# Turning the convolution's blocks at once for two of four tiles

## The chip, the cores and the metric

The kernel runs on one core of a Trainium2 chip. Time is device time in microseconds of one execution, and the times shown are a median of several runs with the lowest and the highest. A core has five instruction queues that run beside each other: TensorE (PE, matrix products; PEld is its weight load), VectorE (DVE), ScalarE (ACT), GpSimd (POOL) and SyncE (SP), which here issues nearly all DMAs. Each queue takes its instructions in order, and an instruction that waits holds up all behind it on its engine. TensorE writes to PSUM, in banks of 128 rows by 512 values; the other data lie in SBUF as 128 rows (partitions).

## The reference

One decoder layer over 2048 rows of 1024 values. What matters here is the convolution group beside the attention group:

```python
    a, gate = jnp.split(u, 2, axis=-1)
    h = a * jax.nn.sigmoid(gate)
    h = lax.conv_general_dilated(
        h, conv_dw[:, None, :].astype(h.dtype), window_strides=(1,),
        padding=[(CONV_WIDTH - 1, 0)],
        dimension_numbers=("NWC", "WIO", "NWC"),
        feature_group_count=D_CONV) + conv_dw_b
    h = jax.nn.silu(layer_norm(h, conv_ln_g, conv_ln_b))
    return h @ w_conv_pw
```

Its result is joined with the attention's, goes through `w_out`, is normed and added to the input, and a dense SwiGLU block (width 2816) follows with its own norm. All is float32; products are made of three products of split operands.

## The kernel before

The 2048 rows are four tiles of 512 (t = 0 to 3). Stage A(t) makes the input projections of a tile, 14 groups of products (`proj`), and writes the gated values of the four blocks of 128 channels to DRAM (glu_scr). Beside it run other stages as side lanes: B(t) is the attention (tags tr, p, kz, ql), U folds the pointwise weights of the convolution into w_out, C(t) is the convolution, W(t) is the output projection with the norms. After them come the stages H, F and G, the SwiGLU block, for tiles 0 and 1 and then for 2 and 3. In the profile a buffer's name carries its stage: fc@C is a buffer of tag fc used by stage C.

The convolution of a tile has two parts.

- `stage_taps(t)` (line 554) works with channels as partitions. For each block c of 128 channels it loads the gated values (glu@C), makes y (fc@C, 128 x 512) with one multiply and 30 multiply-adds on VectorE, all recorded as line 94, and stores y to y_scr in DRAM (line 565).
- `stage_tail(t)` (line 568) loads the four blocks back (line 577) and turns them (`turner`, line 545): four transposes of 128 x 128 on TensorE into the one bank ct (line 549), and a copy by ScalarE into 128 columns of each of the four quarters of yt (line 550). yt then has rows as partitions and 512 channels beside each other.
- `conv_tail` (line 583) takes mean and variance over the channels (line 589), an inverse root on GpSimd, norms in place (line 597), and for each block c turns it back (line 601, bank ct again), makes tanh th and the linear value v in two buffers fc (lines 603, 605), joins them on VectorE (line 606) and stores v to mixT in DRAM (line 607).

mixT holds the eight blocks of 128 values that W(t) multiplies with w_out: four of the attention (line 520) and four of the convolution. W(1), after stage A, loads the attention's four blocks of tile 1 into a buffer of tag yt (line 705) and splits them (hl@W, line 708).

How many buffers a tag has is fixed: glu 2, fc 3, yt 1, ct one bank, tr three banks, mm four. A buffer is given on when the last instruction that uses it is done, a store to DRAM when it has landed.

The order on each engine is made when the program is built. A planner takes the instructions by priority, which follows the order in which they are written out, and by its own clock of when operands and buffers are ready. Main stages run through generators that say how long a piece takes; each lane gets credit at its rate (0.7 for the taps of tile 0, 1.1 for tile 1, lane `lc`; 2.0 for the tails of tiles 0 and 1, lane `ld`), and writes out pieces while it has credit. The taps are written with a priority 100 places behind and are tied to projections so as to keep pace (`dve`, line 92). A tail begins at least CS = 10 of these units after its taps (line 1368). By these rates tile 0's tail is written out while the first block of tile 1 is, and tile 1's second block comes behind it.

Of the kernel before, what the change touches and what calls it, by code (L numbers as in the profile page):

```python
# [17 lines left out]
AF = mybir.ActivationFunctionType  # L18
ALU = mybir.AluOpType
# [6 lines left out]
P = 128  # L26
T = 512
# [10 lines left out]
def layer_kernel(ctx, tc, x, xT, cols, rows, sinks, relb, onehot, w_in, w_pw, w_out, w_gate, w_up, w_down, out):  # L38
    nc = tc.nc
# [9 lines left out]
    def nm(s):  # L49
        uid[0] += 1  # L50
        return f"{s}@{lab[0]}_{uid[0]}"
# [3 lines left out]
    def t_(tag, shape, dt=F32):  # L55
        return sb.tile(list(shape), dt, tag=tag, name=nm(tag), bufs=BUFS[tag])
# [4 lines left out]
    def f2(tag, shape=(P, T)):  # L61
        return t_(tag, shape)
# [4 lines left out]
    def sm(n, dt=F32):  # L67
        kind = "A" if lab[0][0] == "G" else lab[0][0]
        return sb.tile([P, 8], dt, tag="sm" + kind, name=nm("sm"), bufs=16)[:, 0:n]
# [9 lines left out]
    act = nc.scalar.activation  # L79
# [12 lines left out]
    def dve(op):  # L92
        def emit(*args, **kw):
            r = op(*args, **kw)  # L94
            if not paced[0]:
                pace["main"] = r.ins
            elif pace["main"] is not None and pace["main"] is not pace["tied"]:
                tc.add_manual_dep(
                    r.ins,
                    pace["main"].name,  # L100
                    mybir.DependencyInfo(mybir.DependencyClass.NoSync, mybir.DependencyReason.DATA),
                    reason="conv taps keep pace with the projections",
                )
                pace["tied"] = pace["main"]
            if paced[0] and made["rows"]:
                made["new"] = True
                tc.add_manual_dep(
                    r.ins,
                    made["rows"][min(made["at"], len(made["rows"]) - 1)].name,
                    mybir.DependencyInfo(mybir.DependencyClass.NoSync, mybir.DependencyReason.DATA),  # L110
                    reason="conv taps keep pace with the products",
                )
                made["at"] += TIE
            return r

        return emit

    stt = dve(nc.vector.scalar_tensor_tensor)
# [25 lines left out]
    def rsqrt(ssq, n, mean_over, beside_taps=True):  # L144
        v = sm(n)
        y = sm(n)
        t = sm(n)
        vts(v, ssq, 1.0 / mean_over, EPS, ALU.mult, ALU.add)
        vts(y.bitcast(I32), v.bitcast(I32), 1, None, ALU.logical_shift_right)
        vts(y.bitcast(I32), y.bitcast(I32), -1, 0x5F3759DF, ALU.mult, ALU.add)  # L150
        for _ in range(3):
            if beside_taps:
                ptt(t, y, y, ALU.mult)
                ptt(t, t, v, ALU.mult)
                nc.gpsimd.tensor_scalar(t, t, -0.5, 1.5, ALU.mult, ALU.add)
                ptt(y, t, y, ALU.mult)
            else:
                vtt(t, y, y, ALU.mult)
                stt(t, v, -0.5, t, ALU.mult, ALU.mult)
                stt(y, t, 1.5, y, ALU.add, ALU.mult)  # L160
        return y
# [56 lines left out]
    lnh = cst.tile([P, 8], F32, name="lnh")  # L218
# [6 lines left out]
    mixT = dr.tile([KC, P, S], F32, name="mixT")  # L225
# [17 lines left out]
    y_scr = dr.tile([4, P, S], F32, name="y_scr")  # L243
# [290 lines left out]
    def conv_in(t, c):  # L534
        g = t_("glu", (P, 576))[:, 0 : HALO + T]
        if t == 0:
            nc.vector.memset(g[:, 0:HALO], 0.0)
            nc.sync.dma_start(g[:, HALO:], glu_scr[c, :, 0:T])
        else:
            nc.sync.dma_start(g, glu_scr[c, :, t * T - HALO : (t + 1) * T])  # L540
        y = f2("fc")
        vts(y, g[:, 0:T], dwh[:, c, 0:1], dwb[:, c : c + 1], ALU.mult, ALU.add)
        return g, y

    def turner(yt, ycs):
        def turn(c):
            b = ct()
            for s in range(4):
                nc.tensor.transpose(b[:, s * P : (s + 1) * P], ycs[c][:, s * P : (s + 1) * P], ident)
            act(yt[:, :, c * P : (c + 1) * P], b.rearrange("p (s c) -> p s c", c=P), AF.Copy)  # L550

        return turn

    def stage_taps(t):
        L = f"C{t}"
        for c in range(4):
            while f"g{t}{c}" not in started:
                yield None
            lab[0] = L
            g, y = conv_in(t, c)  # L560
            for j in range(1, TAPS):
                stt(y, g[:, j : j + T], dwh[:, c, j : j + 1], y, ALU.mult, ALU.add)
                yield 0.68
                lab[0] = L
            nc.sync.dma_start(y_scr[c, :, t * T : (t + 1) * T], y)
            yield 0.68

    def stage_tail(t):
        L = f"C{t}"
        lab[0] = L  # L570
        yt = t_("yt", (P, 4, 4 * P))
        ycs = []
        turn = turner(yt, ycs)
        for c in range(4):
            lab[0] = L
            y = f2("fc")
            nc.sync.dma_start(y, y_scr[c, :, t * T : (t + 1) * T])
            ycs.append(y)
            turn(c)
            yield 0.5  # L580
        yield from conv_tail(t, yt)

    def conv_tail(t, yt):
        L = f"C{t}"
        lab[0] = L
        mv = sm(8).rearrange("p (s a) -> p s a", a=2)
        for s in range(4):
            st = sm(6)
            nc.vector.bn_stats(st, yt[:, s])
            nc.vector.bn_aggr(mv[:, s], st)  # L590
        r = rsqrt(mv[:, :, 1], 4, 1.0)
        nmr = sm(4)
        stt(nmr, mv[:, :, 0], -1.0, r, ALU.mult, ALU.mult)
        yield YL if t < 2 else YL2
        lab[0] = L
        for s in range(4):
            act(yt[:, s], yt[:, s], AF.Identity, scale=r[:, s : s + 1], bias=nmr[:, s : s + 1])
        for c in range(4):
            b = ct()
            for s in range(4):  # L600
                nc.tensor.transpose(b[:, s * P : (s + 1) * P], yt[:, s, c * P : (c + 1) * P], ident)
            th = f2("fc")
            act(th, b, AF.Tanh, scale=lnh[:, c : c + 1], bias=lnh[:, 4 + c : 5 + c])
            v = f2("fc")
            act(v, b, AF.Identity, scale=lnh[:, c : c + 1], bias=lnh[:, 4 + c : 5 + c])
            stt(v, th, 1.0, v, ALU.add, ALU.mult)
            nc.sync.dma_start(mixT[4 + c, :, t * T : (t + 1) * T], v)
            yield YZ
            lab[0] = L

# [33 lines left out]
    bias = []  # L644
# [720 lines left out]
    for t in range(NT):  # L1365
        lc.add(f"T{t}", stage_taps(t))
    for t in range(2):
        ld.add(f"C{t}", stage_tail(t), lambda t=t: since(lc, f"T{t}", CS))
# [51 lines left out]
    lc.rates["T3"] = RC3  # L1420
    ws, ops = (2, 3), {}
    lw.add("C2", stage_tail(2))
    lw.add("W2", stage_w(2, "mid", ["ql", "chl"], ["chl", "yt"], tr))
    lw.add("C3", stage_tail(3), lambda: since(lc, "T3", CS))
    lw.add("W3", stage_w(3, "mid", ["ql", "chl"], ["chl", "yt"], tr, norm=lambda g: lw.add("N3", g)))
    lw.add("B11.2", stage_h_plain(ws, ops, "B11", 0))
# [71 lines left out]
```

## Time and profile before

| | |
|---|---|
| median of 3 runs | 1985.41 us (1983.29 to 1989.4) |
| profiled execution | 1988.67 us, span 1986.6 us |
| mean granted TensorE clock | 0.992 |
| taps of tile 0, first to last | 44.3 to 236.4 us of the span |
| taps of tile 1, first to last | 181.8 to 430.4 us |
| tail of tile 0, first load to last store | 180.9 to 292.4 us |
| tail of tile 1, first load to last store | 363.3 to 486.9 us |
| stage A, last product | about 485 us |

The span goes from the first to the last instruction of one execution recorded by the profiler. Busy times of engines overlap. A wait is given with the engine and line that waited and what ended it; "mm@A L85" is an instruction on tag mm in stage A that line 85 recorded. PEclk is the share of the full TensorE clock that was granted in a stretch.

### The profile page before, as it was taken

Reading aid. Unit: us, or ns where it says so; the run is one execution under the profiler, and the core shown is the slowest. Engines: PE = TensorE matmul, PEld = TensorE weight load, DVE = VectorE, ACT = ScalarE, POOL = GpSimd, SP = SyncE. Lnnn points to the kernel's source line nnn. Section 1 sums busy time; section 2 is a strip of 40 time slices with the busy share of each in tenths; the row PEclk is TensorE's granted clock in tenths of the full one; section 3 lists DMA queues with packets and bytes.
Section 4 is the critical chain, followed back from the end, with each engine's and each line's share of the span. In section 5 each row is a group of like instructions: output and inputs, shape, how many; then the busy total and the mean of one; then the engine's idle time right before and its main releaser. Section 6 shows DMA issues by size and latency. Waiting matters only on the chain.

```text
span 1986.6 us, 26669 instructions
## 1 busy us (share of the span) xinstructions
PE 1930.2 (97%) x8730; PEld 1542.3 (78%) x8730; DVE 1460.2 (73%) x2578; ACT 955.2 (48%) x1878; POOL 336.4 (17%) x415
## 2 busy tenths in 40 slices
PE   8999999998999999899999999989999999999997
PEld 6777767776777778778888778768888888888886
DVE  5999969986875898888658975766666665455557
ACT  5455454436737633334355466556634433345443
POOL 4011111003121200000000110144423332311003
PEclk9999999999999999999999999989999999999999
DMA  8797757669659867885477788797844542466664
GB/s 312 253 316 234 228 176 242 213 198 306 203 191 353 290 216 237 285 267 181 154 236 251 266 302 282 270 315 244 289 149 165 170 164 81 143 232 194 210 196 144
DMA packets 229403, 454.56 MB, mean 229 GB/s; under 512 B 22632, under 2 KB 48400, under 8 KB 229264
## 3 DMA queue, kind: packets, MB, share of 16 engines
q1 hardware_dynamic: 211024, 426.64, 64.5%
q10 hardware_dynamic: 18240, 26.22, 3.6%
q8 instruction: 69, 1.13, 0.2%
q14 instruction: 70, 0.57, 0.1%
HBM read 331.65 MB, written 121.12 MB: 228 GB/s over the span
## 4 chain that ended last, share of the span: by engine, by line
PE 43%; DMA 10%; DVE 9%; issue 3%; POOL 2%; ACT 2%; SPq 1%; DVEq 0%; ACTq 0%; POOLq 0%
PE mm@F L85 29%; PE mm@G L85 12%; DVE fc@C L94 2%; PE tr@W L85 2%; DMA gb@F<-keeps 1%; DVE hl@G L94 1%; DMA mids<-fa@F 1%; DMA fa@G<-mids 1%; DMA td<-fc@G 1%; DVE w@F L94 1%; DMA fc@G<-w_down 1%; DMA wx@G<-w_down 1%; DVE fa@F L94 1%; DVE chl@F L94 1%; DMA mixT<-fc@C 1%
## 5 line engine op out<-in xcount | busy, mean ns | idle before, releaser
L94 DVE SCALAR_TENSOR_TENSOR fc@C<-glu@C,colt,fc@C 128x512 f32<-128x512 f32 x480 | 356.5, 760 | 2.9
L85 PE MATMUL mm@F<-hl@H,w@F 128*128 128x512 f32 x1056 | 253.0, 390 | 3.3 <-ACT mm@F L919 2.0
L85 PE MATMUL mm@G<-hl@G,hl@G 128*128 128x512 f32 x924 | 232.6, 397 | 11.2 <-ACT hl@G L792 7.7
L85 PEld LDWEIGHTS mm@F<-hl@H,w@F 128*128 128x128 f32 x1056 | 197.5, 188 | 46.3 <-ACT mm@F L919 3.7
L85 PEld LDWEIGHTS mm@G<-hl@G,hl@G 128*128 128x128 f32 x924 | 173.0, 190 | 51.7 <-ACT hl@G L792 9.0
L85 PE MATMUL mm@A<-hl@A,w@A 128*128 128x512 f32 x840 | 206.5, 395 | 4.2 <-ACT w@A L127 1.9
L792 ACT ACTIVATE w@F<-chl@F 128x512 fp32r<-128x512 f32 x220 | 135.4, 625 | 142.1 <-PE mm@F L85 131.5
L85 PE MATMUL mm@G<-w@G,hl@G 128*128 128x512 f32 x876 | 199.4, 389 | 0.0
L85 PEld LDWEIGHTS mm@G<-w@G,hl@G 128*128 128x128 f32 x876 | 164.4, 188 | 34.1
L85 PEld LDWEIGHTS mm@A<-hl@A,w@A 128*128 128x128 f32 x840 | 155.4, 188 | 42.2 <-ACT w@A L127 2.6
L94 DVE TENSOR_TENSOR w@F<-chl@F,w@F 128x512 fp32r<-128x512 f32 x198 | 144.8, 735 | 35.9 <-ACT w@F L792 35.3
L85 PE MATMUL mm@F<-ql@H,w@F 128*128 128x512 f32 x528 | 128.4, 391 | 9.2 <-ACT mm@F L1026 5.0
L85 PE MATMUL mm@F<-mid@H,w@F 128*128 128x512 f32 x528 | 131.7, 396 | 0.0
L85 PE MATMUL mm@F<-p@H,w@F 128*128 128x512 f32 x528 | 129.4, 390 | 0.0
L85 PE MATMUL mm@F<-x@H,w@F 128*128 128x512 f32 x528 | 125.7, 391 | 0.0
L85 PEld LDWEIGHTS mm@F<-ql@H,w@F 128*128 128x128 f32 x528 | 98.8, 188 | 31.6 <-ACT mm@F L1026 6.4
L494 POOL TENSOR_SCALAR_AFFINE_SELECT p@B<-p@B 128x512 f32<-128x512 f32 x62 | 57.6, 938 | 374.0 <-ACT p@B L492 372.7
L85 PEld LDWEIGHTS mm@F<-mid@H,w@F 128*128 128x128 f32 x528 | 100.0, 190 | 21.9 <-ACT fa@F L1047 0.5
L85 PEld LDWEIGHTS mm@F<-p@H,w@F 128*128 128x128 f32 x528 | 99.5, 188 | 21.0 <-ACT at@F L1040 0.2
L85 PEld LDWEIGHTS mm@F<-x@H,w@F 128*128 128x128 f32 x528 | 98.6, 188 | 21.5 <-issue 0.8
L127 ACT ACTIVATE w@A<-raw@A 128x512 fp32r<-128x512 f32 x110 | 67.4, 625 | 93.5 <-PE mm@A L85 54.8
L94 DVE TENSOR_TENSOR w@G<-raw@G,w@G 128x512 fp32r<-128x512 f32 x73 | 51.5, 705 | 68.1 <-ACT w@G L792 66.8
(302 smaller groups left out, 3300.6 us busy)
## 6 DMA issues: line engine op xcount, KB each, us to landing
mids<-fa@F SPq DMA_DIRECT2D x154, 256.0 KB, 2.8
raw@A<-w_in SPq DMA_DIRECT2D x55, 512.0 KB, 4.7
w@A<-lo_in SPq DMA_DIRECT2D x84, 256.0 KB, 3.6
fc@G<-mids SPq DMA_DIRECT2D x77, 256.0 KB, 3.5
fa@G<-mids SPq DMA_DIRECT2D x75, 256.0 KB, 4.6
gb@F<-keeps SPq DMA_DIRECT2D x72, 256.0 KB, 3.9
w@W<-fold SPq DMA_DIRECT2D x32, 512.0 KB, 5.1
chl@F<-w_gate SPq DMA_DIRECT2D x22, 512.0 KB, 4.1
```

Of the source, the lines that this page charges most:

```text
L85: r = nc.tensor.matmul(*args, **kw)
L94: r = op(*args, **kw)
L127: act(w[:, 0], raw, AF.Copy)
L494: nc.gpsimd.affine_select(out=pg[:, kb].rearrange("p (i q) -> p i q", q=P), in_=pg[:, 1].rearrange("p (i q) -> p i q", q=P), compare_op=AL ...
L792: act(w[:, 0], x, AF.Copy)
```

## The change

For tiles 0 and 1 a finished block y is no longer stored to y_scr and loaded back. `stage_taps` takes the tile's yt when its first block is done, and turns each block right behind its last tap. `stage_tail` for these tiles then starts with `conv_tail`. In `conv_tail`, for all four tiles, the value v is written into the 128 columns of yt that were just turned back, no longer into a buffer fc, and the store to mixT reads it there. Tiles 2 and 3 still go through y_scr.

```diff
+    turns = {}
+
     def stage_taps(t):
...
-            nc.sync.dma_start(y_scr[c, :, t * T : (t + 1) * T], y)
+            if t < 2:
+                if c == 0:
+                    turns[t] = t_("yt", (P, 4, 4 * P))
+                turner(turns[t], {c: y})(c)
+            else:
+                nc.sync.dma_start(y_scr[c, :, t * T : (t + 1) * T], y)
             yield 0.68
 
     def stage_tail(t):
         L = f"C{t}"
         lab[0] = L
+        if t < 2:
+            yield from conv_tail(t, turns[t])
+            return
...
-            v = f2("fc")
-            act(v, b, AF.Identity, scale=lnh[:, c : c + 1], bias=lnh[:, 4 + c : 5 + c])
-            stt(v, th, 1.0, v, ALU.add, ALU.mult)
-            nc.sync.dma_start(mixT[4 + c, :, t * T : (t + 1) * T], v)
+            v = yt[:, :, c * P : (c + 1) * P]
+            four = lambda a: a.rearrange("p (s c) -> p s c", c=P)
+            act(v, four(b), AF.Identity, scale=lnh[:, c : c + 1], bias=lnh[:, 4 + c : 5 + c])
+            stt(v, four(th), 1.0, v, ALU.add, ALU.mult)
+            nc.sync.dma_start(four(mixT[4 + c, :, t * T : (t + 1) * T]), v)
             yield YZ
```

The counts of taps, transposes and of ScalarE's and VectorE's instructions stay as they are.

## The prediction

> **What bounds the kernel now.** I read the page's sums first, then the busy time by stretch, then who waits for whom, then the order of time around the waits.
>
> ```profile
> span 1986.6 us, 26669 instructions
> PE 1930.2 (97%) x8730; PEld 1542.3 (78%) x8730; DVE 1460.2 (73%) x2578; ACT 955.2 (48%) x1878; POOL 336.4 (17%) x415
> ```
>
> TensorE is busy in all but 56 us. Nothing in the change takes a matmul away, so all that it can win or lose are gaps of TensorE. Where they lie is shown by the busy time in stretches (columns: length, busy time of PE, PEld, DVE, ACT, POOL, then PE's clock, DMA share, GB/s):
>
> ```profile
> 44.00:245.00 201.00, 198.25 (x966) 153.58 (x966) 192.97 (x410) 96.50 (x228) 20.42 (x29) 1.00 0.77 258
> ...
> 250.00:284.00 34.00, 34.00 (x158) 23.95 (x157) 15.68 (x46) 19.65 (x47) 6.50 (x17) 1.00 0.54 175
> ...
> 481.00:490.00 9.00, 4.87 (x30) 3.71 (x29) 6.27 (x11) 3.57 (x7) 0.00 (x0) 0.88 1.04 396
> 490.00:495.00 5.00, 3.55 (x17) 3.02 (x18) 4.96 (x16) 2.19 (x4) 0.00 (x0) 0.52 1.08 362
> 495.00:560.00 65.00, 65.00 (x312) 46.39 (x311) 51.90 (x132) 38.24 (x102) 8.20 (x8) 1.00 0.67 220
> 560.00:1986.00 1426.00, 1385.66 (x6134) 1133.08 (x6132) 992.03 (x1550) 667.44 (x1211) 244.78 (x264) 0.99 0.67 223
> ```
>
> The convolution of tiles 0 and 1 runs from 44 to 487 us. In it TensorE is full but for one hole, 481 to 495, where it lacks 4.13 + 1.45 = 5.6 us and what it does is done at half clock (0.52). The list of waits names it, and what the turned loads cost today:
>
> ```profile
> PE tr@B L85 <- DVE sm@B L454: 5.6, 1, 5.6
> ...
> PE ct@C L549 <- DMA fc@C<-y_scr: 1.4, 2, 1.0
> ```
>
> The hole in order of time (start, length, engine; in brackets the idle time before it and what ended it):
>
> ```profile
> 476.66 0.38 SPq L607 DMA_DIRECT2D mixT<-fc@C  x1
> ...
> 480.55 0.37 SPq L705 DMA_DIRECT2D yt@W<-mixT  x1
> ...
> 483.66 0.55 DVE L94 TENSOR_SCALAR fc@C<-glu@C,colt 128x512 f32<-128x512 f32 x1 [7.43 <-DMA mixT<-fc@C]
> ...
> 486.17 0.68 DVE L94 SCALAR_TENSOR_TENSOR fc@C<-fc@C,fc@C 128x512 f32<-128x512 f32 x1
> ...
> 486.88 0.33 SPq L607 DMA_DIRECT2D mixT<-fc@C  x1
> ...
> 490.69 1.67 ACT L708 ACTIVATE hl@W<-yt@W 128x512 fp32r<-128x512 f32 x3 [4.69 <-DMA yt@W<-mixT]
> ...
> 491.45 1.65 PE L85 MATMUL tr@B<-kz,ql@A 64*128 64x256 f32 x12 [5.59 <-DVE sm@B L454]
> ...
> 493.03 7.45 PE L85 MATMUL mm@W<-w@W,hl@W 128*128 128x512 f32 x28
> ```
>
> Two chains end here. First, VectorE stands 7.43 us before the first instruction of a block of tile 2: its buffer (tag fc, three of them) is still being stored to mixT by tile 1's tail (issued 476.66). Work queued behind it, the score reductions of B3 that free the banks tr, comes late, and TensorE waits 5.59 us. Second, output projection W1 needs its activations: their load into yt goes out at 480.55, right after the tail's last transposes out of yt, ScalarE gets them at 490.69, and the products start at 493.03. Mending the first chain alone brings little.
>
> **The change part by part.** *The round trip through y_scr.* Eight stores and eight loads go (issues per line, SP's own, for all 16 of the four tiles; last column the median time to landing):
>
> ```profile
> y_scr<-fc@C SPq DMA_DIRECT2D x16, 256.0 KB, 3.3
> mixT<-at@B ACTq DMA_DIRECT2D x16, 256.0 KB, 2.5
> fc@C<-y_scr SPq DMA_DIRECT2D x16, 256.0 KB, 4.8
> mixT<-fc@C SPq DMA_DIRECT2D x16, 256.0 KB, 5.2
> ```
>
> That is 16 x 256 KB = 4.2 MB and 16 places in SP's queue; the transfers were beside other work, so the bytes are worth nothing by themselves. What counts is how long the turn stood behind the last tap:
>
> ```profile
> 236.38 0.32 SPq L565 DMA_DIRECT2D y_scr<-fc@C  x1
> ...
> 244.08 0.66 PE L549 MATMUL ct@C<-ident,fc@C 128*128 128x128 f32 x4 [1.04 <-DMA fc@C<-y_scr]
> ...
> 284.06 0.61 DVE L94 TENSOR_SCALAR fc@C<-glu@C,colt 128x512 f32<-128x512 f32 x1 [5.69 <-DMA mixT<-fc@C]
> ...
> 288.67 1.64 PE L85 MATMUL mm@U<-chl@U,mid@U 128*128 128x512 f32 x6 [0.79 <-DVE chl@U L94]
> ...
> 298.10 2.08 PE L85 MATMUL mm@A<-hl@A,w@A 128*128 128x512 f32 x8 [0.63 <-DVE mb@U L94]
> ```
>
> ```profile
> 430.43 0.32 SPq L565 DMA_DIRECT2D y_scr<-fc@C  x1
> ...
> 439.28 0.65 PE L549 MATMUL ct@C<-ident,fc@C 128*128 128x128 f32 x4
> ...
> 452.78 2.93 ACT L597 ACTIVATE yt@C<-yt@C,sm@C,sm@C 128x512 f32<-128x512 f32 x4 [0.57 <-DVE sm@C L94]
> ```
>
> Tile 0: 244.08 - 236.38 = 7.7 us; tile 1: 439.28 - 430.43 = 8.85 us. Without DRAM the transposes stand in TensorE's queue where the plan has the block finished. How far TensorE is behind VectorE there, I take from a pair of the same form, the normalised probabilities and their transposes:
>
> ```profile
> 198.75 1.28 DVE L94 TENSOR_TENSOR p@B<-p@B,sm@B 128x512 f32<-128x512 f32 x2
> ...
> 203.67 0.60 PE L491 MATMUL tr@B<-ident,p@B 128*128 128x128 f32 x4
> ```
>
> 203.67 - 200.03 = 3.6 us. So the tails start 7.7 - 3.6 = 4.1 and 8.85 - 3.6 = 5.2 us earlier, counted from the last tap.
>
> *The turns themselves.* The same 32 transposes and 8 copies as before, moved ahead in TensorE's and ScalarE's queues:
>
> ```profile
> L549 PE MATMUL ct@C<-ident,fc@C x64: 270/272/329, 193.2 to 1187.5; 128*128 128x128 f32 x64
> ...
> L550 ACT ACTIVATE yt@C<-ct@C x16: 577/597/600, 195.4 to 1187.8; 128x512 f32<-128x512 f32 x16
> ...
> L605 ACT ACTIVATE fc@C<-ct@C,lnh x16: 763/772/783, 266.8 to 1221.8; 128x512 f32<-128x512 f32 x16
> ```
>
> Their busy time is unchanged: 0. New is that each group waits for taps on VectorE and not for a load. From below that costs 0 (TensorE is 3.6 us behind), from above the 1.04 us of the one turn that did make TensorE wait, eight times: 8.3 us. I take 0.2 us each, 1.6 in all, nearer to the pair's row; VectorE is full there (192.97 of 201 us), so it isn't nothing. Behind a waiting transpose stand the projections of stage A, all of TensorE's work.
>
> *Values into the columns of yt.* L550 already writes such columns (597 ns), so L605 keeps its 772 ns. For VectorE's multiply no row has columns; between 0 and double its time, 8 x 0.68 = 5.4 us in two tails, it lies on an engine with 18.3 us to spare in 250 to 284: 0. The stores of mixT go out in runs of 512 B, not 2 KB. ScalarE's stores of at into the same mixT have such runs and land in 2.5 us, the tail's in 5.2, so 0; the ends are 2.5 and, as the longest store-like row here, the 10.1 us from 480.55 to 490.69.
>
> The Trainium skill speaks against this part: DMA: Bandwidth & Descriptors, Why small descriptors are slow (HBM only), gives a fixed overhead of about 3 cycles per packet beside 32-byte beats. By it a 512-byte run would cost 19 cycles for 16 and a 2 KB run 67 for 64, an estimate of some 13% more, or 0.7 us on a landing of 5.2; the row of at does not bear it out.
>
> *Buffers.* The tail takes four buffers of fc, not twelve, and none of them waits for a store. VectorE's waits of 5.69 and 7.43 us end. Tile 1's second block, written out in the plan behind tile 0's tail, starts earlier than 284.06 by the 4.1 us and by the 5.69; VectorE has the room (15.68 of 34 us busy). I take 6 us of it as surviving to tile 1's last tap: 424 for 430.43. In return the block finished first in tile 1 keeps its buffer until tile 0's last store has landed and yt is free (about 285): one buffer of three, and the tail needs one.
>
> In the tails of tiles 2 and 3 only the columns change. The buffer yt is next wanted there by a load of the very values that the tail stores, which waits for their landing anyway: 0.
>
> *The new wait.* yt is now held until the store of tile 1's last piece has landed, and W1's load of yt comes behind it. Today that piece is made at 486.17. Earlier taps take 6 us off, the missing round trip 5.2, and of VectorE's 7.43 us I count 3: made at 472, stored at 473, landed (5.2) at 478, against 480.55 for the load today. With its own 10.1 us the load arrives at 488; TensorE would be ready at 485.86 + 1.65 = 487.5 (the end of its work before the gap, 491.45 - 5.59, and the 12 score products). What is late next is thus this load, by 0.5 us; I take 1.2 with what follows on ScalarE.
>
> *Sum.* Hole at 491: -5.6. Half clock: 3.55 us of work at 0.52 becomes 1.85: -1.7. The waits of 1.04, 0.79 and 0.63, all behind the loads and VectorE's wait: -2.5. Turns +1.6, load of yt +1.2. Together -7.0 us. The profiled execution took 1988.67 us (span 1986.6 and 2.1 around it), so 1981.7 for its like; it is 3.3 us above the median of the runs, 1985.41, from which I forecast 1978.4.
>
> **The rivals.** *yt is let go too late (slower).* If tile 1's tail doesn't move, its last store is issued at 486.88 and lands at 492.1; the load goes 11.5 us later than now, the products of W1 start at 504.6, and the gap is 17 us for 5.8: with the small waits gone 1985.4 + 11.3 - 2.5 = 1994.2. It decides when that landing passes 480.55; it already eats the gain from about 477.4 (487.5 - 10.1). For it: not to lose I need 11.5 of the 14.2 us that I put together (6 + 5.2 + 3), and the tail's last two stores stand 10 us apart today (476.66, 486.88). Against it: both waits for mixT are gone for certain.
>
> *The hole stays.* The landing falls near 480: TensorE stops at W1's products, not at tr, and starts them at 493 as now. Only the 2.5 us less the 1.6 of turns are won: 1984.5.
>
> *Turns stop TensorE (slower).* If VectorE is behind the plan by x at each of eight turns, 8x is lost; at x = 1.1 the gain is gone (7.0 + 1.6 over 8), at the 7.7 us of the round trip it would be 60 us. With 2 us: 1978.4 - 1.6 + 16 = 1992.8. For it: VectorE is 96% busy until 245. Against it: TensorE never waits for VectorE in that stretch, by the list.
>
> *Another plan behind it.* All buffers and times of the plan from 245 us on shift, and the 40.3 us that TensorE lacks from 560 on (1426 - 1385.66) fall anew. Nothing says which way; a sixth of them, 6 us, either side: 1972 or 1984 on top of the forecast.
>
> **How the numbers follow.** From no change a measurement of this kernel tells about 0.3%, 6 us. Forecast as worked out 0.42 (own range 1974 to 1982; 0.33 over the bound, 0.09 within it); yt too late 0.15, slower; the hole stays 0.12, the same; turns stop TensorE 0.14 (0.10 slower, 0.04 the same); another plan 0.17 (0.08 faster, 0.04 the same, 0.05 slower). Faster 0.41, same 0.29, slower 0.30. The range: low 1972 from the better plan, high 1995 to take in yt too late and two microseconds at each turn.
>
> **What would show it.** In the changed kernel's profile: no wait of VectorE for mixT before 500 us; transposes of the turn within some 4 us of the last tap, TensorE's waits at them under 2 us in sum; tile 1's last tap before 428; the load of yt for W1 out before 480; no gap over 2 us and no clock under 1.0 between 481 and 495. Wrong it would be by a load of yt later than 481, by waits of TensorE for taps of a microsecond and more, or by gaps from 560 on over 46 us.

## The result, and the profile after

The changed kernel took 1998.0 us (median of 5, 1993.83 to 1998.56), the kernel before 1987.25 (median of 5, 1983.29 to 1989.4): a ratio of 1.0058, 95% interval 1.0043 to 1.0073. It is slower by 0.6%; the forecast was 1978.4. The profiled execution took 1996.4 us. The first line of the page, and the busy time by stretch (length, then PE, PEld, DVE, ACT, POOL, PE's clock, DMA share, GB/s), changed kernel:

```profile
span 1994.5 us, 26648 instructions
```

```profile
44.00:245.00 201.00, 200.98 (x978) 155.54 (x978) 193.80 (x409) 96.69 (x230) 18.96 (x31) 1.00 0.75 250
245.00:350.00 105.00, 105.00 (x498) 76.77 (x497) 85.92 (x198) 55.24 (x131) 16.70 (x27) 1.00 0.64 209
350.00:430.00 80.00, 80.00 (x383) 59.03 (x383) 75.04 (x174) 29.23 (x86) 6.93 (x8) 1.00 0.58 183
478.00:484.00 6.00, 4.44 (x40) 3.27 (x40) 4.88 (x23) 3.73 (x7) 0.00 (x0) 0.94 0.99 378
484.00:502.00 18.00, 8.39 (x44) 6.30 (x43) 12.41 (x35) 8.31 (x26) 0.00 (x0) 0.50 0.91 283
502.00:508.00 6.00, 6.00 (x18) 4.77 (x18) 5.29 (x16) 4.04 (x8) 1.63 (x2) 0.56 0.40 137
...
560.00:1994.00 1434.00, 1393.68 (x6157) 1139.80 (x6156) 993.36 (x1555) 668.81 (x1213) 245.76 (x264) 0.99 0.67 223
```

The same view of the kernel before, in the stretches of the hole, and before it:

```profile
245.00:350.00 105.00, 103.58 (x492) 75.24 (x490) 86.01 (x190) 55.53 (x130) 17.40 (x28) 1.00 0.65 214
350.00:430.00 80.00, 79.42 (x369) 57.22 (x366) 72.70 (x163) 30.40 (x88) 6.89 (x8) 1.00 0.63 202
478.00:484.00 6.00, 6.00 (x30) 4.96 (x29) 0.34 (x1) 5.42 (x8) 0.00 (x0) 1.00 1.01 395
484.00:502.00 18.00, 12.41 (x65) 9.35 (x63) 17.82 (x45) 6.11 (x21) 0.00 (x0) 0.81 0.92 312
502.00:508.00 6.00, 6.00 (x36) 4.86 (x34) 5.96 (x20) 6.00 (x15) 0.00 (x0) 1.00 0.69 242
```

Two things are to be seen. Up to 430 us the change does more than it was given: TensorE lacks 0.02 us from 44 to 430, where it lacked 4.75 (2.75, 1.42 and 0.58), so the turns cost it nothing. Then the hole is not closed but doubled: from 478 to 508 TensorE lacks 11.2 us instead of 5.6, and its clock is at half. Counted in work at full clock (busy time by clock, an estimate), those 30 us held 6.00 + 12.41 x 0.81 + 6.00 = 22.05 us before and 4.44 x 0.94 + 8.39 x 0.50 + 6.00 x 0.56 = 11.73 now. That is 10.3 lost; less the 4.7 won it leaves 5.6.

The hole in order of time, changed kernel (start, length, engine; in brackets the idle time and what ended it):

```profile
484.23 2.02 SPq L799 DMA_DIRECT2D fa@H<-hn_scr  x4
484.94 0.68 DVE L94 SCALAR_TENSOR_TENSOR yt@C<-fc@C,yt@C 128x512 f32<-128x512 f32 x1
...
488.94 0.98 SPq L618 DMA_DIRECT2D mixT<-yt@C  x1
...
495.61 0.36 SPq L716 DMA_DIRECT2D yt@W<-mixT  x1
...
500.99 2.19 ACT L719 ACTIVATE hl@W<-yt@W 128x512 fp32r<-128x512 f32 x4 [4.37 <-DMA yt@W<-mixT]
501.67 3.78 PE L85 MATMUL mm@W<-w@W,hl@W 128*128 128x512 f32 x8 [4.11 <-ACT hl@W L719]
```

VectorE's waits for mixT are gone. But W1's load of yt goes out at 495.61 instead of 480.55, behind the landing of tile 1's last store (issued 488.94), and W1's first product starts at 501.67 instead of 493.03. That store's value was made at 485.6 (484.94 + 0.68) and lay 3.3 us: SP's queue stood behind the loads fa@H of stage H (484.23), which had waited 4.0 us for stores to hn_scr (in DRAM) to land.

Behind the hole, two marks show the rest: the first transpose of stage H into tr, and the first product of stage G.

```profile
637.06 0.60 PE L810 MATMUL tr@H<-ident,fc@H 128*128 128x128 f32 x4
1012.95 1.52 PE L85 MATMUL mm@G<-hl@G,hl@G 128*128 128x512 f32 x6
```

```profile
642.63 0.60 PE L821 MATMUL tr@H<-ident,fc@H 128*128 128x128 f32 x4
1024.36 0.84 PE L85 MATMUL mm@G<-hl@G,hl@G 128*128 128x512 f32 x3
```

The first fence is before, the second after. To the first mark the changed kernel loses 5.6 us, the hole; from mark to mark 381.7 us stand for 375.9, another 5.8, in a stage that the change doesn't touch; and from there to the end it wins 3.5 back (spans 1994.5 and 1986.6).

### The profile page after: what moved, and what is told of

Same layout as the page of the kernel before. It is cut to its first block, busy times and chain, and to the rows that moved or that the text cites. A ratio compares the mean times of both kernels' runs of the same rounds, so it can differ in the third digit from the quotient of the medians.

```text
span 1994.5 us, 26648 instructions
## 1 busy us (share of the span) xinstructions
PE 1937.1 (97%) x8730; PEld 1549.0 (78%) x8730; DVE 1460.4 (73%) x2578; ACT 953.7 (48%) x1878; POOL 334.8 (17%) x415
## 4 chain that ended last, share of the span: by engine, by line
PE 74%; DMA 10%; DVE 10%; issue 3%; POOL 2%; ACT 1%; SPq 1%; DVEq 0%; ACTq 0%; POOLq 0%
PE mm@F L85 33%; PE mm@A L85 15%; PE mm@G L85 11%; PE mm@W L85 5%; PE tr@B L85 4%; DVE fc@C L94 2%; PE tr@W L85 2%; DVE hl@G L94 1%; DMA mids<-fa@F 1%; PE mm@U L85 1%; DMA fa@G<-mids 1%; DMA td<-fc@G 1%; DVE w@F L94 1%; PE tr@B L491 1%; DMA mixT<-yt@C 1%
```

## The experiments

Theory H: the loss is yt, held until tile 1's last store has landed. Rivals: theory T, the turns put tile 1's taps late, so the hole opens wherever v goes; and theory F, the planner's order behind 580 us came out worse by chance.

**The turns alone (e1).** v goes back into a buffer fc in all tails.

```diff
-            v = yt[:, :, c * P : (c + 1) * P]
+            v = f2("fc")
```

> The turns at once are kept, the values v of all tails go into a buffer fc as before the change. Theory H (yt held): the loss at 483 to 508 comes from yt being kept until tile 1's last store of mixT has landed. Then the load of yt for W1 goes out right behind tile 1's last back-transposes (482 in the changed kernel, not 495.6), W1's first product starts some 12 us earlier, the time TensorE lacks between 478 and 508 falls from 11.2 us (6 - 4.44 and 18 - 8.39) to 6 or less, and the time is 1988 to 1992. Theory T (the turns at once put tile 1's taps late, last tap 441 for 430): the load still comes by 482, but the waits of VectorE for mixT are back, and the time is 1992 to 1998. Theory F (the stages behind 640 were planned anew and cost 5.5 us): gaps from 560 on stay within 6 us of the changed kernel's or fall elsewhere, and the time may come out either side by that much.

2001.13 us, ratio 1.0059 (1.0044 to 1.0074). Theory H's numbers were not met, and the time lies above the ranges of both H and T, although TensorE lacks only 6.8 us from 478 to 508 (23.23 of 30 us busy) for the changed kernel's 11.2. The last turn of tile 1 came at 449.16 (441.34 in the changed kernel), and yt was held all the same, in another way: the tail's pieces waited for buffers fc that were still being stored.

```profile
491.98 0.78 ACT L615 ACTIVATE fc@C<-ct@C,lnh 128x512 f32<-128x512 f32 x1 [1.34 <-DMA mixT<-fc@C]
...
492.81 1.11 PE L611 MATMUL ct@C<-ident,yt@C 128*128 128x128 f32 x4 [2.82 <-ACT fc@C L615]
...
493.96 0.37 SPq L715 DMA_DIRECT2D yt@W<-mixT  x1
```

So the late tail is a cause beside the held yt: theory T has a part.

**The columns alone (e2).** The kernel before, with v in yt and the round trip kept.

```diff
-            v = f2("fc")
+            v = yt[:, :, c * P : (c + 1) * P]
```

> The kernel before with one part of the change alone: v goes into the columns of yt for all four tails; the round trip through y_scr stays for all tiles. Theory H: VectorE's waits of 5.69 and 7.43 us for mixT end, but yt is kept until tile 1's last store lands, so its load for W1 goes out behind 487 (before: 480.55), W1's products start at 499 or later, and the time is 1990 to 1996. Theory T: without the turns tile 1's last tap comes by 424 to 428, its last store by 481, the load leaves by 486, and the time is 1980 to 1987: then the columns are the part that gains and the turns the part that loses.

1995.29 us, ratio 1.0028 (1.0017 to 1.0040): theory H, within its range.

```profile
277.81 0.55 DVE L94 TENSOR_SCALAR fc@C<-glu@C,colt 128x512 f32<-128x512 f32 x1
...
426.17 0.32 SPq L565 DMA_DIRECT2D y_scr<-fc@C  x1
...
483.35 0.45 SPq L608 DMA_DIRECT2D mixT<-yt@C  x1
...
490.56 0.74 SPq L706 DMA_DIRECT2D yt@W<-mixT  x1
```

Tile 1's second block starts at 277.81 for 284.06, and its last tap ends 4.3 us earlier (426.17 for 430.43): the gain of buffers that the prediction counted on is there, when the turns are not. Yet the load of yt leaves 10 us later than before, since it now stands behind the landing of the last store (issued 483.35).

**Only tile 0 turned at once (e3)**, columns in all tails.

```diff
-            if t < 2:
+            if t < 1:
```

> Tile 0 is turned at once, tile 1 goes through y_scr as before the change; v goes into the columns of yt for all tails. Theory H: the load of yt for W1 still waits for tile 1's last store, which stands where the taps of tile 1 put it; leaves at 490 or later, 1992 to 1998. Theory T (it is tile 1's own turns, or tile 2's first block beside tile 1's last, that made the last tap 441): last tap by 431, the load leaves by 487, 1982 to 1990.

2001.8 us, ratio 1.0068 (1.0052 to 1.0085). Tile 1's last block was stored at 439.32, as late as with both tiles turned, and W1's load left at 497.95. So tile 0's turns alone put tile 1's taps late; tile 1's own add nothing that can be seen here. The time lies above the ranges of both theories.

**Tile 1's v back in fc (e4)**, all else as changed.

```diff
+            if t != 1:
                 v = yt[:, :, c * P : (c + 1) * P]
...
+            else:
+                v = f2("fc")
```

> The changed kernel with one thing undone: v of tile 1 goes into a buffer fc, the other tails keep the columns of yt. Theory H: yt comes free with tile 1's last back-transposes, the load for W1 leaves at 483 or earlier (495.61 in the changed kernel), TensorE lacks 6 us or less between 478 and 508 (11.2), and the time is the changed kernel's less 5 to 8 us: 1990 to 1993. Rival (the hole is due to the late taps of tile 1, wherever v goes): the load leaves no more than 5 us earlier and the time stays within 3 us of the changed kernel's.

1994.34 us, ratio 1.0026 (1.0015 to 1.0037). By medians it is 3.7 us under the changed kernel, short of the 5 to 8 expected; by the two ratios, each to the kernel before on the same chip, it is 0.3%, some 6 us.

```profile
484.88 2.02 SPq L805 DMA_DIRECT2D fa@H<-hn_scr  x4
...
488.02 0.38 SPq L624 DMA_DIRECT2D mixT<-fc@C  x1
488.49 0.38 SPq L722 DMA_DIRECT2D yt@W<-mixT  x1
```

The load goes 7.1 us earlier than in the changed kernel, no more: yt was free after the transposes of 483.84, but in SP's queue the load now stands behind the third store. That store's value was there by 484.0; the store itself stood behind stage H's loads (484.88), which had waited 4.1 us for stores to hn_scr.

**W1's load freed from yt (e5, e6).** W1 takes its first activations into two buffers of tag chl, in the changed kernel (e5) and in the kernel before (e6).

```diff
-    run(stage_w(1, "mid", ["hl", "chl"], ["yt", "yt"], mm,
+    run(stage_w(1, "mid", ["hl", "chl"], ["chl", "yt"], mm,
```

> The changed kernel, with W1's first activations loaded into two buffers of tag chl instead of the one yt, so that tile 1's tail can't hold that load. Theory H (yt held): the load leaves before 480, W1's first product comes before 493, the time TensorE lacks between 478 and 508 falls from 11.2 to under 4 us, the half clock there (483 to 507) goes, and the time falls by 6 to 9 us against the changed kernel's 1998: 1989 to 1992. Theory F (the other half of the loss is the stage between the first tr@H and the first mm@G, 375.9 us before the change and 380.8 to 384.9 in all five kernels with a changed plan): that stretch stays 380 to 386 us here too, so the hole alone doesn't bring the kernel under the time before. Rival (the load waits for something else, attention's stores or SP's queue): it still leaves after 485 and the time stays within 3 us of 1998.

> The kernel before, with the same one edit: W1's first activations go into tag chl. It tells how much of the hole in the kernel before hung on yt. Theory H: the load leaves some us before 480.55, W1's products start before 493.03, but VectorE's 7.43 us wait for mixT and TensorE's 5.59 us behind it stay; 1983 to 1988 if the stage from tr@H to mm@G keeps its 376 us. Theory F: that stretch becomes 380 to 386 us as in every kernel with a changed plan, and the time is 1988 to 1993 although the hole is no larger.

e5: 1980.29 us, ratio 0.9962 (0.9949 to 0.9976), faster than both and below the 1989 to 1992 expected. e6: 1994.61, ratio 1.0032 (1.0020 to 1.0044). In e5 the taps and turns stand as in the changed kernel (last turn 441.44 for 441.34); what differs is this, by busy time and in order of time:

```profile
478.00:508.00 30.00, 29.61 (x164) 22.96 (x163) 23.82 (x66) 22.41 (x51) 0.00 (x0) 1.00 0.96 313
```

```profile
454.78 0.37 SPq L716 DMA_DIRECT2D chl@W<-mixT  x1
...
480.10 0.50 PE L85 MATMUL mm@W<-w@W,hl@W 128*128 128x512 f32 x1
...
491.71 0.36 SPq L618 DMA_DIRECT2D mixT<-yt@C  x1
```

Tile 1's last store is even later (491.71), and it costs nothing, since nothing of W1's first half waits for yt. The hole and its half clock are gone; the first tr@H comes at 629.83, 12.8 us before the changed kernel's and 7.2 before that of the kernel before. Theory H is shown for the hole: once the load doesn't wait for yt the hole is gone, though tile 1's taps and tail are as late as in the changed kernel. e6 has no hole either (30.00 of 30.00 us busy), though VectorE still waits 3.13 us for mixT there. But its TensorE stops 4.85 us at 624.87, its first tr@H comes at 637.8, no earlier than in the kernel before (637.06), and it takes 384 us from mark to mark: a closed hole isn't yet a gain.

**The plan behind 580 us (e7 to e10, e14).** One rate that leaves the plan of tiles 0 and 1 as it is, that of the lane S0, is 0.95 or 0.85 instead of 0.9.

```diff
-    lh.rates = {"N1": 1.2, "S0": 0.9, "H0": 1.2}
+    lh.rates = {"N1": 1.2, "S0": 0.95, "H0": 1.2}
```

> The kernel before, with one rate changed that has nothing to do with the convolution: the lane that writes out the sums of stage H (S0) runs at 0.95 instead of 0.9, so the plan is the same up to about 580 us and made anew behind it. Theory F (the plan of the stage from tr@H to mm@G is a lucky one, any other costs 4 to 9 us): that stretch rises from 375.9 to 380 or more, and the time is 1991 to 1996. Rival (only what the change does to buffers or to the convolution's later blocks lengthens that stage): it stays within 2 us of 375.9, and the time within 3 us of 1988.4.

> The kernel before with the S0 lane at 0.85 instead of 0.9, a second draw of its plan behind 580 us beside the one at 0.95 (2000.4 us for 1988.5). If the plan at 0.9 is a lucky one among many, this too is slower than before, by 3 to 12 us: 1991 to 2000. If 0.95 was the unlucky one, it is within 3 us of 1988.4. With the two draws of the changed kernel it tells what part of the change's 10 us belongs to the hole at 490 and what part to the draw.

> The changed kernel with the S0 lane at 0.95 instead of 0.9: everything up to about 580 us stays as it is in the changed kernel (hole at 483 to 507 included), the plan behind it is drawn anew. Theory H with plan luck: the first tr@H comes at 642 to 645 as in the changed kernel, the stage from there to the first mm@G takes anything from 376 to 385 us (the bounds of the plans seen), and the time is 1990 to 2008. Rival (the change itself lengthens that stage, by what it does to buffers): the stage stays 381 to 385 us.

> The same at 0.85: a second draw of the plan behind 580 us for the changed kernel. First tr@H at 642 to 645, the stage from there to mm@G 376 to 385 us, 1990 to 2008 us.

> The changed kernel with W1's first activations in tag chl, and the S0 lane at 0.95. At 0.95 the kernel before took 2000.4 us and the changed one 2007.5. Theory H: first tr@H at 629 to 631 as with chl at 0.9, and whatever the draw behind, less than the 2007.5 by 8 to 16 us: 1991 to 2000. If the gain of the run with chl (1980.29) was a lucky draw of the plan behind, it is 2003 or more.

Marks are starts in one profiled execution of each kernel, "to the end" is from the first mm@G to the end of the span; the ratio is to the kernel before at 0.9, on the same chip.

| kernel | rate | first tr@H | to first mm@G | to the end | median | ratio (interval) |
|---|---|---|---|---|---|---|
| before | 0.9 | 637.1 | 375.9 | 973.6 | 1987.25 | 1 |
| before (e7) | 0.95 | 639.2 | 378.8 | 979.5 | 2000.43 | 1.0065 (1.0052 to 1.0078) |
| before (e10) | 0.85 | 635.8 | 385.4 | 982.8 | 2004.44 | 1.0081 (1.0065 to 1.0097) |
| changed | 0.9 | 642.6 | 381.7 | 970.1 | 1998.0 | 1.0058 (1.0043 to 1.0073) |
| changed (e8) | 0.95 | 643.4 | 378.5 | 983.5 | 2007.52 | 1.0101 (1.0085 to 1.0118) |
| changed (e9) | 0.85 | 644.2 | 376.1 | 985.8 | 2006.56 | 1.0090 (1.0073 to 1.0107) |
| with chl (e5) | 0.9 | 629.8 | 376.5 | 969.9 | 1980.29 | 0.9962 (0.9949 to 0.9976) |
| with chl (e14) | 0.95 | 634.4 | 381.1 | 986.9 | 1998.65 | 1.0061 (1.0039 to 1.0083) |

The times of e7 and e10 came out above the ranges expected, those of e8, e9 and e14 inside theirs; e14's first mark is 3 us later than expected. Theory F holds in part. The stage between the marks takes 376 to 385 us in these kernels, with no order by the change: means of 380.0 before and 378.8 after. So the 5.8 us that the changed kernel lost there look like a draw; what makes a plan longer there isn't shown. The first mark comes at 635.8 to 639.2 in the three kernels without the change and at 642.6 to 644.2 in the three with it: 6.0 us apart in the mean, the hole. The spans of the three differ by 5.9 in the mean. By medians the whole difference is 10.8 us at 0.9, some 7 at 0.95 and some 2 at 0.85, where the intervals overlap; only the hole's share is the change's own.

But the rate is not a neutral one. The kernel holds the lane of the taps, lc, until S0 is written out (line 1412 of the kernel before), and at both other rates the last block of tile 3's convolution is stored some 20 us later, counted from the first mm@G. It is 1170.3 - 1013.0 = 157.3 us in the kernel before and 1195.1 - 1018.0 = 177.1 in e7 (all stores of y_scr with least, median and longest ns, and the starts of the first and the last; first the kernel before, then e7):

```profile
L565 SPq DMA_DIRECT2D y_scr<-fc@C x16: 319/320/425, 112.8 to 1170.3; - x16
```

```profile
L565 SPq DMA_DIRECT2D y_scr<-fc@C x16: 319/320/913, 113.8 to 1195.1; - x16
```

In all ten kernels at 0.9 (before, changed, e1 to e6, e11 and e13) that distance is 155.7 to 157.9 us, and the stretch to the end 968.6 to 973.6; in the five at other rates they are 176.7 to 178.6 and 979.5 to 986.9. So what these rates cost lies for a good part in the last stretch, in every one of them, and says little on whether the plan at 0.9 is a lucky one. That the later block is the cause there isn't shown.

Nor is e5's gain over the kernel before safe: at 0.95 they are alike (1.0061 and 1.0065). Over the changed kernel it has 18 and 9 us.

**Columns and chl, without turns (e11).**

> The columns of yt alone, with the round trip through y_scr kept, and W1's first activations in tag chl. With the columns alone tile 1's last tap came at 426.17 (430.43 before, 440.9 with the turns). If the turns at once add nothing to the gain, the hole is gone here too (TensorE lacks under 2 us from 478 to 508), the first tr@H comes at 628 to 633, and the time is 1978 to 1990, the width being the draw of the plan behind. If the turns are what made the changed kernel with chl fast (1980.29), this stays at 1988 or above with its first tr@H behind 634.

1984.65 us, ratio 0.9990 (0.9981 to 1.0000): the hole is gone (30.00 of 30.00), but the first tr@H comes at 637.3. The time is that of the first case, the mark that of the second. The last product of stage A starts at 481.20 here and at 475.69 in e5: 5.5 us of e5's lead lie ahead of the hole, with the turns.

**A second bank for the tail (e13).** Pieces 1 and 3 of the tails of tiles 0 and 1 are turned back into a bank tr.

```diff
-            b = ct()
+            b = tr() if t < 2 and c % 2 else ct()
```

> The changed kernel, with the back-transposes of pieces 1 and 3 of the tails of tiles 0 and 1 in a bank of tag tr instead of ct, so that a piece need not wait until ScalarE has read the one before. If the one bank spaces the pieces (6 to 8 us in the changed kernel's tile 1), they come in pairs, the last store of tile 1 leaves some 6 us earlier (by 483), the load of yt for W1 by 489, and TensorE lacks 8 us or less from 478 to 508 instead of 11.2. If TensorE's queue spaces them, or SP's queue holds the stores (made at 484.94, issued at 488.94 in the changed kernel), the load stays behind 492 and the time within 3 us of 1998 but for the draw of the plan behind.

1988.7 us, ratio 1.0004 (0.9993 to 1.0015), 9.3 us under the changed kernel. It moved far more than was expected. Tile 0's tail, first the changed kernel, then e13:

```profile
271.15 0.60 PE L611 MATMUL ct@C<-ident,yt@C 128*128 128x128 f32 x4
...
277.44 0.60 PE L611 MATMUL ct@C<-ident,yt@C 128*128 128x128 f32 x4
...
283.77 0.60 PE L611 MATMUL ct@C<-ident,yt@C 128*128 128x128 f32 x4
...
285.87 0.53 DVE L94 TENSOR_SCALAR fc@C<-glu@C,colt 128x512 f32<-128x512 f32 x1
...
289.08 0.37 SPq L618 DMA_DIRECT2D mixT<-yt@C  x1
...
290.19 0.60 PE L549 MATMUL ct@C<-ident,fc@C 128*128 128x128 f32 x4
```

```profile
266.88 0.78 ACT L613 ACTIVATE fc@C<-ct@C,lnh 128x512 f32<-128x512 f32 x1 [2.42 <-PE ct@C L611]
267.56 0.77 ACT L613 ACTIVATE fc@C<-tr@C,lnh 128x512 f32<-128x512 f32 x1
...
270.78 0.44 SPq L618 DMA_DIRECT2D mixT<-yt@C  x1
273.48 1.00 DVE L94 TENSOR_SCALAR fc@C<-glu@C,colt 128x512 f32<-128x512 f32 x2
273.91 0.60 PE L549 MATMUL ct@C<-ident,fc@C 128*128 128x128 f32 x4
```

The pieces come in pairs instead of 6.3 us apart, tile 0's tail ends 18 us earlier (270.78 for 289.08), tile 1's second block starts with it (273.48 for 285.87), the last turn of tile 1 comes at 398.58 for 441.34, and its last store at 431.27: W1's load left at 435.16, far from any hole. What it won it partly gave back in a stop of 4.84 us at 464.92, where TensorE waits for ScalarE's copies of the attention. Two things limit what this run shows. Of the 43 us by which the last turn comes earlier, only 12 are the earlier start of the second block; the others lie in the blocks' own pace. And the plan is another one from tile 0's tail on: the first transpose back already comes at 257.29 for 260.92. So the spacing goes with the one bank, and a tail that ends early leaves no hole; what the bank alone is worth isn't shown.

**Tile 1 alone turned at once (e12).** Tile 0 goes through y_scr, with the columns in all tails.

```diff
-            if t < 2:
+            if t == 1:
```

This kernel gives no time: its instructions wait for each other without end (a deadlock). So tile 1's turns without those of tile 0 stay unmeasured.

## Why the prediction was wrong

The rival "yt is let go too late" came true, with a chance of 0.15, and "another plan behind it" beside it; together they gave 1998, past the 1994.2 of the first and past the range. At the first mark the loss is 5.6 us, less than the first rival's 11.3 - 2.5 = 8.8; what brings it to 1998 comes behind.

- *The round trip.* Right: no turn waits for DRAM, and tile 1's last turn (441.34) stands directly behind the last taps. Only tile 1's first block waits, for yt: its taps end at 249.1, its turn comes at 290.19.
- *The turns themselves, 1.6 us.* Nothing was paid (200.98 of 201 us busy).
- *The small waits, -2.5.* They came to -4.7.
- *The columns, 0.* Right. The stores of mixT still land in 5.2 us, so the 0.7 us estimated from the Trainium skill (DMA: Bandwidth & Descriptors, Why small descriptors are slow) did not show; VectorE's multiply took 688 ns (issues of a line with the median time to landing, and the instructions of tile yt with the least, median and longest ns, changed kernel).

```profile
mixT<-yt@C SPq DMA_DIRECT2D x16, 256.0 KB, 5.2
```

```profile
L94 DVE SCALAR_TENSOR_TENSOR yt@C<-fc@C,yt@C x16: 681/688/696, 267.1 to 1233.9; 128x512 f32<-128x512 f32 x16
```

- *Buffers: this is the step that failed.* "Tile 1's second block ... starts earlier than 284.06" and "I take 6 us of it as surviving to tile 1's last tap: 424 for 430.43". It started at 285.87, and the last taps ended near 440. The prediction had named what stands against it (the first finished block of tile 1 keeps its buffer until tile 0's last store has landed), and counted it as harmless: one buffer of three. But with the turns at once, tile 1's second block starts with the end of tile 0's tail, in the changed kernel (285.87) as in e13 (273.48), and the length of that tail goes with its pieces, one behind the other through one bank. The columns alone, without the turns, gave most of the gain forecast (426.17). The late start is the smaller part, though: the second block stands 1.8 us behind the kernel before and the fourth 2.8 (357.06 for 354.24), but the last tap some 10. The rest is the fourth block's pace beside the first block of tile 2. That one started 6.1 us behind it (11.5 before) and was stored as the fourth was turned, where it had been stored 17 us behind it (447.73 for 430.43). First the changed kernel, then the kernel before:

```profile
440.86 0.38 SPq L572 DMA_DIRECT2D y_scr<-fc@C  x1
...
441.34 0.60 PE L549 MATMUL ct@C<-ident,fc@C 128*128 128x128 f32 x4
```

```profile
447.73 0.38 SPq L565 DMA_DIRECT2D y_scr<-fc@C  x1
```

VectorE is busy 148.0 of the 156 us from 285 to 441 (146.7 before), so the two blocks share an engine that is nearly full; why the planner gives tile 2's more isn't shown.

- *The new wait, +1.2.* The tail's length came out as forecast: it took 484.94 - 441.34 = 43.6 us from last turn to last piece, against the 46.9 - 3 = 43.9 that the forecast had used (486.17 - 439.28, less 3). That is luck in part, for in e5, from the same last turn, it took 49.6 (441.44 to 491.00). The sum was fed with the wrong tap, and it left out SP's queue: the piece made at 485.6 was issued at 488.94, behind loads of stage H. The load that waits for its landing left at 495.61, where the forecast had the landing at 478; at 480.55 the sign turns.
- *The hole, -5.6 and -1.7.* It became 10.3 us of lost work in place of a gain, of which the half clock is a good part (8.39 + 6.00 us busy at 0.50 and 0.56 do 7.6).
- *The gaps from 560 us on.* As forecast, under 46 us: 1434 - 1393.68 = 40.3, the same as before. The stage between the marks alone lacks 18.1 us for 15.2 (384 - 365.88 from 640 to 1024, 373 - 357.84 from 640 to 1013), at a mean clock of 0.98 for 0.99, and later stages lack less.
- *Another plan, 6 us either side.* The size was right for the stage it met (5.8 lost, 3.5 won back). In the ten kernels at the rate 0.9 that stage takes 374.7 to 384.8 us, up to 8.9 above the 375.9 of the kernel before, so as a bound it was a little small. The 12 and 17 us of the other rates are no test of it, since those rates also move tile 3's convolution.

Not settled: why the planner lets tile 2's first block run so close beside tile 1's fourth; what makes the stage between the marks longer in one plan than in another; and what tile 1's turns cost without those of tile 0.

## What to carry to other kernels

When an edit saves a buffer by keeping its data in another, ask who takes that other buffer next, and follow the time at which it is let go through every step that leads to it, each with its measured row; here one step of five, moved by some 16 us, turned the sign, and naming another buffer for the next user (one word) took the hole away, though a gain over the kernel before held at only one of two rates. Where a planner orders everything anew, run the same edit under two or three plans, and look first at what else the changed setting moves: the rate of one lane of stage H moved this kernel by 0.65 and 0.8%, more than the edit did, and with it tile 3's convolution by some 20 us.

## What the runs showed of the hardware

The clock fell without a long stop. Busy time in stretches of 2 us, changed kernel:

```profile
480.00:482.00 2.00, 1.19 (x14) 0.98 (x13) 1.84 (x11) 1.45 (x2) 0.00 (x0) 1.00 1.02 397
482.00:484.00 2.00, 1.25 (x12) 0.91 (x11) 2.00 (x11) 1.16 (x2) 0.00 (x0) 0.83 0.92 322
...
502.00:504.00 2.00, 2.00 (x6) 1.52 (x6) 2.00 (x4) 2.00 (x5) 0.00 (x0) 0.50 0.01 1
...
506.00:508.00 2.00, 2.00 (x8) 1.65 (x7) 1.29 (x3) 1.26 (x2) 0.01 (x1) 0.69 0.84 274
```

It went to half within 482 to 484, where TensorE was still busy 1.2 of every 2 us and waited at most 0.81 us at a time (481.23, for sm@B), and it came back only within 506 to 508, after more than 4 us of full work. The Trainium skill (TensorE: Matmul & The Clock Gate, Why this matters for your kernels) warns of idle gaps over some 3 us. Here gaps of up to 0.8 us, close together, were enough, and the measurement decides. In the kernel before one stop was enough, after some 2 us: TensorE stood still from 485.86, and the granted clock was 0.98 in the stretch from 486 to 488 and 0.50 from 488 to 490.
